# Pool weights fused between the first value tiles, and 16-row value tiles with high and low parts stacked

## The chip, the cores and the metric

The kernel runs on one core of a Trainium2 chip. Its time is the device time of one execution in microseconds (us). Times of before and after are medians of several executions; a profile is one further execution, recorded by the hardware profiler. The engines are PE (matmul), ACT, DVE and POOL (elementwise work), and SP, which here only issues the transfers (DMAs).

## What is computed

One hybrid decoder layer over 2064 tokens (16 meta tokens and 2048 others), width 1024:

```python
h = layer_norm(concat([meta, x]), ln_in_g, ln_in_b)
q, k, v, f_logit, g_att, u, g_pool = split(h @ w_in)
a = forgetting_attention(q, k, v, f_logit, b_forget) * silu(g_att)   # 16 heads of 64
p = multiscale_pool(u, w_pool, pool_scale) * silu(g_pool)            # 4 groups of 256
y = concat([a, p]) @ w_out
out = layer_norm(2**0.25 * h + y, ln_g, ln_b)[16:]
```

In the pool mixer a trailing mean and then a linear map w_pool act on u, which is itself a projection. Both are linear, so the kernel multiplies the u columns of w_in by w_pool first, group by group, and projects with the product. This is "fusing the pool weights".

## The kernel before

Every float32 matmul is made of three: an operand is split into a high part (rounded to the PE's reduced format by ACT) and a low part (the rest, by a subtraction on DVE or POOL), and high x high, high x low and low x high are summed (`mm3`, `split`). All compute instructions go through a helper at line 86 that fixes the order on PE, DVE, ACT and POOL as written; every profile row therefore has line L86, and is told apart by its tiles. Transfers on SP are not fixed by it: their order comes from the framework's own planner.

The change touches the first phase, up to the value projection (lines 189 to 401):

- **Fusing.** `fuse_load(g)` fetches the raw weights of pool group g: wpool (128x512, 256 KB) and two tiles of the transposed u columns (128x1024, 512 KB each) into a pool of their own, `fz`. `fuse_split` makes high and low parts (ph, pl, uh, ul), `fuse_mm(g)` runs 48 matmuls of 256 columns in four PSUM tiles and stores the product to `wupd`. The four groups run one after the other at the start (line 355); the splits of the next group, the LayerNorm of a token tile and the splits of the value weights stand between the matmuls. Then `fz` is closed and its memory goes to `hh` and `hl`.
- **LayerNorm.** `ln_load(i)` fetches a tile of 128 tokens (i = -1: the 16 meta tokens); `ln_norm(i)` takes statistics on DVE (bst, mv, rs, nb), normalizes on ACT, and applies gain and bias on POOL (xt<-xt,g_bc and xt<-xt,b_bc). `ln_turn(i)` transposes the tile on PE (tr<-ident,xt) and splits it into `hh` (ACT) and `hl` (DVE), columns 16+128i to 144+128i.
- **Value tiles.** `v_tile(half, wts, kt)` multiplies 128 tokens by 512 value columns: 24 matmuls of 512 columns (d<-wvh,hh and its two partners), then a split into a `vs` tile (two buffers, `vslot`) and a 512 KB store to `vd`. 2064 tokens make 16 full tiles and one of 16 rows; the 16-row tile takes 24 matmuls as well. Half 0 runs inside the loop at line 375 that also loads tile i+4, transposes tile i+1 and normalizes tile i+3. Half 1 follows at line 396.
- **Weights of half 1.** Eight 256 KB pieces through three staging buffers (`wst`); three are fetched ahead, one is split ahead of the 16-row tile of half 0, the other seven behind it.

After the value tiles come forget logits, the other projections, attention, output projection and the closing LayerNorm; none of that is touched.

Of the kernel before, what the change touches and what calls it, by code (L numbers as in the profile page):

```python
# [16 lines left out]
P = 128  # L17
NM = 16
# [22 lines left out]
def kernel(  # L41
# [147 lines left out]
    with ExitStack() as vscope:  # L189
        vpool = pool(vscope, "vpool")  # L190
# [21 lines left out]
        def ln_norm(i):  # L212
# [11 lines left out]
            nc.vector.scalar_tensor_tensor(  # L224
                out=nb[:n], in0=mv[:n, 0:1], scalar=-1.0, in1=rs[:n], op0=ALU.mult, op1=ALU.mult
            )
            nc.scalar.activation(
                out=xt[:n], in_=xt[:n], func=AF.Identity, scale=rs[:n], bias=nb[:n]
            )
            for op, row in ((ALU.mult, g_bc), (ALU.add, b_bc)):  # L230
                nc.gpsimd.tensor_tensor(out=xt[:n], in0=xt[:n], in1=row[:n], op=op)
# [26 lines left out]
        def v_tile(half, wts, kt):  # L258
            n = min(P, L - P * kt)
            ps = dense()  # L260
            sl = slice(P * kt, P * kt + n)
            for k in range(KT):
                mm3(ps[:n], hh[:, k, sl], hl[:, k, sl], wts[k][0], wts[k][1], k == 0, k == KT - 1)
            vs = vslot().rearrange("p (h a e) -> p h a e", h=8, a=2)
            pv = ps[:n].rearrange("p (h e) -> p h e", e=DH)
            split(vs[:n, :, 1, :], vs[:n, :, 0, :], pv)
# [5 lines left out]
        fscope = ExitStack()  # L272
        fz = pool(fscope, "fz", side="right")

        def fuse_load(g):
            wp = fz.tile([P, 2, 256], F32, tag="wp", name="wp", bufs=4)
            dma(wp, wpool[g])
            us = [wp]
            for k in range(2):
                us.append(fz.tile([P, D], F32, tag="wu", name="wu", bufs=8))  # L280
                dma(us[-1], wut[2 * g + k])
            return us

        def fuse_split(us, r):
            def one(i, u):
                shape, tag = ([P, 2, 256], "p") if i == 0 else ([P, D], "u")
                h_, l_ = (
                    fz.tile(shape, F32R, tag=tag + t, name=tag + t, bufs=2 if i == 0 else 4)
                    for t in "hl"
                )  # L290
                split(h_, l_, u, nc.gpsimd if i == 2 else None)
                r.append((h_, l_))

            return [lambda i=i, u=u: one(i, u) for i, u in enumerate(us)]

        def fuse_mm(g, ws, us, pieces):
            raw = [
                f32(vslot()) if g == 3 else fz.tile([P, D], F32, tag="o", name="o", bufs=6)
                for _ in range(2)
            ]  # L300
            os = [t.rearrange("p (k b e) -> p k b e", k=4, b=2) for t in raw]
            n = -(-len(pieces) // 4)

            def evac(kp, ps):
                pv = ps.rearrange("p (a b e) -> p a b e", a=2, b=2)
                dst = os[kp // 2][:, 2 * (kp % 2) : 2 * (kp % 2) + 2]
                if kp % 2:
                    nc.vector.tensor_copy(dst, pv)
                else:
                    nc.scalar.copy(out=dst, in_=pv)  # L310

            last = None
            for kp in range(4):
                ps = dense()
                for s in range(2):
                    dsl = slice(P * (2 * kp + s), P * (2 * kp + s + 1))
                    for k in range(2):
                        mm3(
                            ps[:, 256 * s : 256 * (s + 1)], us[k][0][:, dsl], us[k][1][:, dsl],
                            ws[0][:, k], ws[1][:, k], k == 0, k == 1,  # L320
                        )
                if last:
                    evac(*last)
                last = (kp, ps)
                for f in pieces[n * kp : n * (kp + 1)]:
                    f()
            evac(*last)
            for b in range(2):
                for q in range(2):
                    dma(wupd[2 * g + b][:, 4 * q : 4 * q + 4, :], os[q][:, :, b, :])  # L330
# [3 lines left out]
        raws = {0: fuse_load(0)}  # L334
# [7 lines left out]
        raws[3] = fuse_load(3)  # L342
        ln_load(2)
        sts = deque()
        for k in range(KT):
            sts.append(fz.tile([P, 512], F32, tag="wv", name="wv", bufs=KT))
            dma(sts[-1], wv[0, k])
        dma(wfs, wf)
        dma(bf_t, b_forget)
        dma(psc_t, pool_scale)  # L350
        hot = []
        for f in fuse_split(raws.pop(0), hot):
            f()
        wts = []
        for g in range(4):
            us = hot
            ws = us.pop(0)
            hot = []
            pieces = []
            if g + 1 < 4:  # L360
                pieces += fuse_split(raws.pop(g + 1), hot)
                pieces.append(lambda: ln_norm(g - 1))
            if g >= 2:
                pieces += [lambda: wts.append(wv_split(sts.popleft()))] * 4
            fuse_mm(g, ws, us, pieces)
        fscope.close()
        htp = pool(phase_a, "htp", side="right")
        hh = htp.tile([P, KT, L], F32R, tag="hh", name="hh")
        hl = htp.tile([P, KT, L], F32R, tag="hl", name="hl")
        ln_turn(-1)  # L370
        ln_load(3)
        ln_turn(0)
        ln_norm(2)
        split(wfr[:, :, 0:H], wfr[:, :, 32 : 32 + H], wfs)
        for i in range(NKT):
            if i + 4 < 16:
                ln_load(i + 4)
            if i + 1 < 16:
                ln_turn(i + 1)
            if i + 3 < 16:  # L380
                ln_norm(i + 3)
            if i == 14:
# [8 lines left out]
        wts = wts1  # L391
        for k in range(1, KT):
            wts.append(wv_split(sts.popleft()))
            if k + 3 < KT:
                sts.append(wv_load(1, k + 3))
        for kt in range(NKT):
# [4 lines left out]
            v_tile(1, wts, kt)  # L401

# [824 lines left out]
```

## Time and profile before

| | |
|---|---|
| time before, median of 3 | 2393.3 us (2392.06 to 2394.99) |
| the profiled execution's own time | 2390.21 us |
| its span | 2388.5 us |
| PE busy, share of the span | 2321.6 us, 97% |
| DVE / ACT / POOL busy | 60% / 40% / 30% |

The span runs from the first to the last recorded instruction. PE is TensorE's matmul row; since matmuls overlap, its recorded durations are longer than the distance from one start to the next, and the distance is what counts. "Idle before" a row is the time that its engine waited, with what released it behind the arrow. The granted clock is given as a share of the full 2.4 GHz; 0.5 is the lower level, 1.2 GHz.

### The profile page before, as it was taken

What the parts mean: (1) busy time and instruction counts of PE and PEld (TensorE: products, weight loads), DVE (VectorE), ACT (ScalarE), POOL (GpSimd) and SP (SyncE); (2) the same over time, 40 slices, a digit from 0 to 9 for tenths busy, and PEclk for the clock granted to TensorE, in tenths of its full rate; (3) what the DMA queues carried; (4) which work ended last, traced back from release to release, by engine and by line L of the source; (5) the groups of instructions that cost most, each with busy time, mean ns of one, the idle gap of its engine ahead of it and who ended that gap; (6) DMA issues with size and microseconds to landing.
All of it is one profiled execution on the core that took longest, in us unless ns stands there. A gap on an engine that the chain in (4) does not pass through costs nothing. (4 is left out here: it accounts for less than half of the span.)

```text
span 2388.5 us, 32719 instructions
## 1 busy us (share of the span) xinstructions
PE 2321.6 (97%) x11706; PEld 1922.0 (80%) x11706; DVE 1431.6 (60%) x2116; ACT 959.7 (40%) x1813; POOL 718.1 (30%) x528
## 2 busy tenths in 40 slices
PE   6999999999999999999999999999999999999998
PEld 5778798898988989888887767777777777776787
DVE  6641145644655456545535188787888878778357
ACT  4431221222212212121111387777778777776000
POOL 4730021212313404050001135353453535444000
PEclk8999999999999999999999999999999999999999
DMA  7853231222222222222212576575666657555955
GB/s 255 263 164 97 59 96 61 89 63 82 90 61 90 77 66 85 68 75 86 77 67 79 159 205 190 159 222 164 195 187 198 199 164 227 175 176 152 310 185 167
DMA packets 317506, 333.59 MB, mean 140 GB/s; under 512 B 27744, under 2 KB 241072, under 8 KB 317312
## 3 DMA queue, kind: packets, MB, share of 16 engines
q1 hardware_dynamic: 317344, 331.51, 45.5%
q8 instruction: 92, 1.51, 0.3%
q14 instruction: 70, 0.57, 0.1%
HBM read 207.43 MB, written 124.00 MB: 139 GB/s over the span
## 5 line engine op out<-in xcount | busy, mean ns | idle before, releaser
L86 PE MATMUL d<-hh,wh 128*128 128x412 f32 (+2 forms) x1472 | 561.2, 381 | 0.0
L86 PE MATMUL d<-hl,wh 128*128 128x412 f32 (+2 forms) x1472 | 538.6, 366 | 0.0
L86 PE MATMUL d<-hh,wl 128*128 128x412 f32 (+2 forms) x1472 | 538.6, 366 | 0.0
L86 DVE TENSOR_REDUCE mxs<-mx 128x1 f32<-128x912 f32 (+14 forms) x416 | 358.1, 864 | 279.7 <-PE mx L86 275.2
L86 DVE TENSOR_TENSOR pl<-s,ph 128x512 fp32r<-128x512 f32 (+2 forms) x576 | 374.6, 663 | 166.6 <-ACT s L86 153.5
L86 ACT ACTIVATE ph<-s 128x512 fp32r<-128x512 f32 (+2 forms) x576 | 334.6, 581 | 170.1 <-PE s L86 159.2
L86 PE MATMUL d<-wh,xm 128*128 128x512 f32 x1024 | 352.3, 400 | 5.1 <-DMA xm<-xa 5.1
L86 ACT ACTIVATE s<-s 128x512 f32<-128x512 f32 (+2 forms) x576 | 332.7, 578 | 0.0
L86 PEld LDWEIGHTS d<-hl,wh 128*128 128x128 f32 x1472 | 278.4, 189 | 23.1
L86 PEld LDWEIGHTS d<-hh,wl 128*128 128x128 f32 x1472 | 276.9, 188 | 23.5
L86 PEld LDWEIGHTS d<-hh,wh 128*128 128x128 f32 x1472 | 280.6, 191 | 18.2
L86 PE MATMUL s<-qa,ka 68*128 68x512 f32 (+4 forms) x704 | 258.1, 367 | 18.4 <-DVE pl L86 18.3
L86 POOL TENSOR_TENSOR wl<-wst,wh 128x1024 fp32r<-128x1024 f32 x40 | 96.2, 2405 | 576.0 <-ACT wh L86 575.9
L86 PE MATMUL s<-qb,kb 128*128 128x512 f32 (+4 forms) x704 | 244.8, 351 | 0.0
L86 PE MATMUL xo<-ph,vt 128*128 128x512 f32 (+3 forms) x640 | 232.9, 368 | 0.0
L86 POOL TENSOR_TENSOR tu<-ph 128x512 f32<-128x512 f32 x144 | 191.3, 1330 | 134.6 <-ACT ph L86 116.1
L86 PEld LDWEIGHTS d<-wh,xm 128*128 128x128 f32 x1024 | 192.3, 189 | 42.8 <-issue 4.9
L86 PE MATMUL yo<-pl,vt 128*66 128x512 f32 (+3 forms) x640 | 223.0, 365 | 0.5 <-ACT c L86 0.5
L86 PE MATMUL mx<-ka,qa 66*128 66x512 f32 (+5 forms) x704 | 200.2, 351 | 6.5 <-ACT qa L86 3.9
L86 PE MATMUL d<-wl,xm 128*128 128x512 f32 x512 | 204.3, 399 | 0.0
L86 PEld LDWEIGHTS s<-qa,ka 68*128 68x128 f32 (+1 forms) x704 | 127.7, 181 | 73.3 <-DVE pl L86 31.3
L86 PEld LDWEIGHTS mx<-ka,qa 66*128 66x128 f32 x704 | 133.0, 190 | 23.5 <-ACT qa L86 5.2
(140 smaller groups left out, 3049.2 us busy)
## 6 DMA issues: line engine op xcount, KB each, us to landing
xm<-xp SPq DMA_DIRECT2D x32, 1024.0 KB
xm<-xa SPq DMA_DIRECT2D x20, 1024.0 KB
vd<-vs SPq DMA_DIRECT2D x32, 512.0 KB
vt<-vd SPq DMA_DIRECT2D x64, 256.0 KB
qb<-kqd SPq DMA_DIRECT2D x64, 256.0 KB
xa<-am SPq DMA_DIRECT2D x32, 512.0 KB
xp<-pm SPq DMA_DIRECT2D x32, 412.0 KB
kqd<-lo SPq DMA_DIRECT2D x64, 206.0 KB
```

The costliest lines, as they stand in the source:

```text
L86: return in_order(f(*a, **k))
```

## The change

The pool `fz` goes. `hh` and `hl` are allocated at the start, and the split pool weights are kept in their last 1024 columns, which token tiles 8 and up fill later (`fuse_parts`: sixteen slots, five for a group). Raw pieces pass through the three `wst` buffers as 256 KB pieces (`fuse_feed`); the products are evacuated by ACT alone, 128x1024 at a time, into the `vs` buffers. Group 0 is fused first, from raw tiles that sit in a `wst` and both `vs` buffers; meta and token tile 0 are normalized ahead of its splits, tile 0's gain and bias are on DVE. Value tile 0 follows, and groups 1, 2 and 3 are fused ahead of value tiles 1, 2 and 3; the pieces of group g+1 are split behind the transposes of an iteration. The 16-row tiles use a stack `hs` of 48 columns (high part in 0 to 15, low part in 32 to 47, zeros between): 16 matmuls instead of 24, whose two row groups are added at the end; the low x low product is thereby included. Between the matmuls of the first of them, the weights of half 1 are split; two of these are now staged in another pool (`wq`). The forget weights are loaded and split later.

```diff
+        htp = pool(phase_a, "htp", side="right")
+        hh = htp.tile([P, KT, L], F32R, tag="hh", name="hh")
+        hl = htp.tile([P, KT, L], F32R, tag="hl", name="hl")
...
+        def v_rest(half, wts, hs, each):
+            ps = dense()
+            for k in range(KT):
+                for t in range(2):
+                    mm(
+                        ps[:48], hs[:, k, :], wts[k][t],
+                        start=k == 0 and t == 0, stop=k == KT - 1 and t == 1,
+                    )
+                each(k)
+            vf = wslot("wst")
+            nc.scalar.copy(out=vf[:NM], in_=ps[32:48])
+            nc.vector.tensor_tensor(out=vf[:NM], in0=ps[:NM], in1=vf[:NM], op=ALU.add)
+            v_out(half, NKT - 1, NM, vf[:NM])
...
+        def fuse_parts(g):
+            def slot(i):
+                i += 5 * (g % 3)
+                return (hh, hl)[i // KT][:, i % KT, L - D : L]
...
+        def fuse_feed(g):
+            parts = fuse_parts(g)
+            pieces = [(*parts[0], wpool[g])]
             for k in range(2):
...
+                for c in range(2):
+                    cs = slice(512 * c, 512 * (c + 1))
+                    pieces.append((parts[1 + k][0][:, cs], parts[1 + k][1][:, cs], wut[2 * g + k, :, cs]))
...
+            def step(i):
+                split(pieces[i][0], pieces[i][1], raw[i])
+                if i + 3 < 5:
+                    load(i + 3)
+
+            for i in range(3):
+                load(i)
+            for i in range(5):
+                step(i)
+            return parts
+
+        def fuse_mm(g, f, pieces):
+            ws, *us = f
+            pieces = deque(pieces)
+            for half in range(2):
+                ps = psm.tile([P, 1024], F32, tag="mx", name="fz", bufs=2)
...
+                    if pieces:
+                        pieces.popleft()()
+                o = f32(vslot())
+                nc.scalar.copy(out=o, in_=ps)
...
         ln_load(-1)
-        raws[1] = fuse_load(1)
         ln_load(0)
+        first = [wslot("wst").rearrange("p (k e) -> p k e", k=2), f32(vslot()), f32(vslot())]
+        for st, src in zip(first, (wpool[0], wut[0], wut[1])):
+            dma(st, src)
         bcast_row(g_bc, ln_in_g)
         bcast_row(b_bc, ln_in_b)
-        raws[2] = fuse_load(2)
+        wraw = lnp.tile([P, D], F32, tag="xt", name="wraw", bufs=4)
+        sts = deque(wraw[:, 512 * k : 512 * (k + 1)] for k in range(2))
+        for k in range(2):
+            dma(sts[k], wv[0, k])
+        sts.extend(wv_load(0, k) for k in range(2, 4))
         ln_load(1)
...
+        stats = [ln_stat(i) for i in (-1, 0)]
+        gains = [ln_apply(i, *stats[i + 1], nc.vector if i == 0 else None) for i in (-1, 0)]
+        fz = {0: fuse_parts(0)}
+        for (h_, l_), st in zip(fz[0], first):
+            split(h_, l_, st)
+        for f in gains:
             f()
         wts = []
...
+        def wv_next():
+            k = len(wts)
+            if k + 4 < KT:
+                sts.append(wv_load(0, k + 4))
+            wts.append(wv_split(sts.popleft()))
+
+        fuse_mm(0, fz.pop(0), [wv_next] * 4)
         ln_turn(-1)
+        ln_load(2)
+        ln_turn(0)
         ln_load(3)
-        ln_turn(0)
+        while len(wts) < KT:
+            wv_next()
+        ln_norm(1)
+        fz[1] = fuse_feed(1)
         ln_norm(2)
-        split(wfr[:, :, 0:H], wfr[:, :, 32 : 32 + H], wfs)
-        for i in range(NKT):
+        for i in range(NKT - 1):
+            if i in fz:
+                fuse_mm(i, fz.pop(i), [])
             if i + 4 < 16:
                 ln_load(i + 4)
-            if i + 1 < 16:
+            if 1 <= i < 15:
                 ln_turn(i + 1)
+            if 1 <= i < 3:
+                fz[i + 1] = fuse_feed(i + 1)
             if i + 3 < 16:
                 ln_norm(i + 3)
...
             if i == 14:
                 sts = deque(wv_load(1, k) for k in range(3))
-            if i == 16:
-                wts1 = [wv_split(sts.popleft())]
-                sts.append(wv_load(1, 3))
+            if i == 15:
+                w1 = [wv_split(sts.popleft())]
+                nc.scalar.copy(out=hs[:, :, 0:NM], in_=f32(hh[:, :, L - NM : L]))
+                nc.vector.tensor_copy(hs[:, :, 32:48], f32(hl[:, :, L - NM : L]))
             v_tile(0, wts, i)
-            if i == 15:
+            if i == 0:
+                ln_turn(1)
+            if i == 14:
                 lnscope.close()
                 wq = pool(phase_a, "wq", side="right")
...
+        def each(k):
+            if sts:
+                w1.append(wv_split(sts.popleft()))
+            if k + 5 < KT:
+                sts.append(wv_load(1, k + 5))
+
+        v_rest(0, wts, hs, each)
```

## Rows read from the trace of the kernel before

**Rows 1.** The page of the profile: busy us, share of the span and instructions of each engine.

```profile
PE 2321.6 (97%) x11706; PEld 1922.0 (80%) x11706; DVE 1431.6 (60%) x2116; ACT 959.7 (40%) x1813; POOL 718.1 (30%) x528
```

**Rows 2.** Stretches of the span, one row each: busy time and instructions of each engine, then PE's granted clock, the DMA share and GB/s.

```profile
0.00:60.00 60.00, 39.25 (x232) 35.71 (x233) 40.49 (x51) 29.29 (x45) 29.22 (x22) 0.89 0.75 256
60.00:100.00 40.00, 37.22 (x186) 30.40 (x185) 26.24 (x51) 18.40 (x32) 30.04 (x13) 1.00 0.84 270
166.50:177.40 10.90, 7.61 (x26) 4.34 (x25) 5.20 (x8) 4.61 (x8) 0.00 (x0) 1.00 0.36 103
```

**Rows 3.** Timeline of PE in the first 110 us: start, duration, operation, and idle time before it. d<-ph,uh and its partners are the matmuls of the pool groups, tr the transposes (those of 55.46, 64.31 and 97.44 are token tiles 1, 2 and 7).

```profile
10.61 0.58 PE L86 MATMUL d<-ph,ul 128*128 128x256 f32 x1 [1.63 <-POOL ul L86]
14.84 0.41 PE L86 MATMUL d<-ph,uh 128*128 128x256 f32 x1
15.05 0.36 PE L86 MATMUL d<-pl,uh 128*128 128x256 f32 x1
16.43 0.28 PE L86 MATMUL d<-ph,uh 128*128 128x256 f32 x1
16.55 0.28 PE L86 MATMUL d<-pl,uh 128*128 128x256 f32 x1
27.50 0.58 PE L86 MATMUL d<-ph,uh 128*128 128x256 f32 x1 [4.31 <-DVE o L86]
51.80 0.66 PE L86 MATMUL tr<-ident,xt 16*128 16x16 f32 x8
55.46 1.17 PE L86 MATMUL tr<-ident,xt 128*128 128x128 f32 x8 [1.05 <-DVE hl L86]
64.31 1.09 PE L86 MATMUL tr<-ident,xt 128*128 128x128 f32 x8 [2.12 <-POOL xt L86]
97.44 1.03 PE L86 MATMUL tr<-ident,xt 128*128 128x128 f32 x8
```

**Rows 4.** Groups of instructions up to 260 us, by shape: count | busy us, mean ns of one | idle before them. wv and wst are staged value weights, hl and hh the parts of the transposed tokens.

```profile
L86 POOL TENSOR_TENSOR xt<-xt,b_bc 128x1024 f32<-128x1024 f32 x16 | 39.0, 2438 | 1.3
L86 POOL TENSOR_TENSOR xt<-xt,g_bc 128x1024 f32<-128x1024 f32 x16 | 38.4, 2400 | 36.3 <-ACT xt L86 36.3
L86 DVE TENSOR_TENSOR hl<-tr,hh 128x512 fp32r<-128x512 f32 x32 | 20.5, 680 | 1.2 <-ACT hh L86 1.2
L86 ACT CAST hh<-tr 128x512 fp32r<-128x512 f32 x32 | 17.2, 594 | 1.3 <-PE tr L86 1.3
L86 ACT CAST uh<-wu 128x1024 fp32r<-128x1024 f32 x8 | 8.2, 1045 | 1.9 <-DMA wu<-in_wut_dram 1.9
L86 DVE TENSOR_TENSOR wvl<-wst,wvh 128x512 fp32r<-128x512 f32 x8 | 5.3, 683 | 4.1 <-ACT wvh L86 4.1
L86 ACT CAST wvh<-wst 128x512 fp32r<-128x512 f32 x8 | 4.7, 617 | 4.6 <-DMA wst<-in_wv_dram 4.5
```

**Rows 5.** Timeline of DVE in the first 75 us: start, duration, operation.

```profile
33.82 3.41 DVE L86 TENSOR_TENSOR ul<-wu,uh 128x1024 fp32r<-128x1024 f32 x1
37.15 1.27 DVE L86 BATCH_NORM_STATS2 bst<-xt 128x6 f32<-128x512 f32 x2
54.63 1.29 DVE L86 TENSOR_TENSOR hl<-tr,hh 128x512 fp32r<-128x512 f32 x2 [1.24 <-ACT hh L86]
71.05 0.53 DVE L86 SCALAR_TENSOR_TENSOR nb<-mv,rs 128x1 f32<-128x1 f32 x1
```

**Rows 6.** Timeline of POOL in the first 75 us.

```profile
33.43 2.72 POOL L86 TENSOR_TENSOR xt<-xt,b_bc 128x1024 f32<-128x1024 f32 x1
69.18 2.38 POOL L86 TENSOR_TENSOR xt<-xt,b_bc 128x1024 f32<-128x1024 f32 x1
```

**Rows 7.** Timeline of ACT in the first 75 us: the third split of group 0, and a normalization.

```profile
7.09 1.04 ACT L86 CAST uh<-wu 128x1024 fp32r<-128x1024 f32 x1 [0.76 <-DMA wu<-in_wut_dram]
39.48 1.24 ACT L86 ACTIVATE xt<-xt,nb,rs 128x1024 f32<-128x1024 f32 x1 [0.43 <-DVE nb L86]
```

**Rows 8.** Timeline of ACT from 148 us on: the end of half 0 and the start of half 1.

```profile
166.70 0.57 ACT L86 CAST vs<-d 16x512 fp32r<-16x512 f32 x1 [4.46 <-PE d L86]
175.25 0.62 ACT L86 CAST wvh<-wst 128x512 fp32r<-128x512 f32 x1 [1.42 <-DMA wst<-in_wv_dram]
177.42 0.59 ACT L86 CAST vs<-d 128x512 fp32r<-128x512 f32 x1 [1.55 <-PE d L86]
182.98 0.59 ACT L86 CAST vs<-d 128x512 fp32r<-128x512 f32 x1 [4.97 <-PE d L86]
```

**Rows 9.** Timeline of DVE in the same stretch.

```profile
171.96 1.34 DVE L86 TENSOR_TENSOR wvl<-wst,wvh 128x512 fp32r<-128x512 f32 x2 [2.17 <-ACT wvh L86]
183.60 0.69 DVE L86 TENSOR_TENSOR vs<-d,vs 128x512 fp32r<-128x512 f32 x1 [4.87 <-ACT vs L86]
```

**Rows 10.** Stretches of 0.5 us behind the DVE row of 183.60, when one store of a value tile is the only transfer: the last column is GB/s, the one before it the DMA share.

```profile
185.30:185.80 0.50, 0.50 (x4) 0.38 (x3) 0.00 (x0) 0.00 (x0) 0.00 (x0) 1.00 1.02 294
186.80:187.30 0.50, 0.50 (x4) 0.42 (x3) 0.00 (x0) 0.00 (x0) 0.00 (x0) 1.00 0.53 149
```

**Rows 11.** Timeline of PE at the end of half 1: the first and the last of the 24 matmuls of the 16-row tile.

```profile
260.62 0.40 PE L86 MATMUL d<-wvh,hh 128*16 128x512 f32 x1
265.95 0.39 PE L86 MATMUL d<-wvh,hl 128*16 128x512 f32 x1
```

**Rows 12.** Transfers of the first 100 us: GB/s in 40 slices of 2.5 us.

```profile
GB/s 27 381 338 415 408 405 408 405 401 389 386 343 296 280 4 0 105 0 0 80 286 212 225 356 324 224 243 333 107 300 383 185 370 246 321 224 137 357 236 326
```

More of the change, by code (lines that the diff above doesn't have):

```diff
@@ L210, in ln_load, with ln_stat @@
             xts[i] = xt
-        def ln_norm(i):
+        def ln_stat(i):
             n = NM if i < 0 else P
@@ L229, in ln_norm, with ln_gain @@
             )
+            return lambda: ln_gain(i, eng or nc.gpsimd)
+        def ln_gain(i, eng):
+            n = NM if i < 0 else P
+            xt = xts[i]
             for op, row in ((ALU.mult, g_bc), (ALU.add, b_bc)):
-                nc.gpsimd.tensor_tensor(out=xt[:n], in0=xt[:n], in1=row[:n], op=op)
+                eng.tensor_tensor(out=xt[:n], in0=xt[:n], in1=row[:n], op=op)
+        def ln_norm(i):
+            ln_apply(i, *ln_stat(i))()
         def ln_turn(i):
@@ L256, in wv_split, with v_out @@
             return h_, l_
[L258 to L263, printed above, removed]
+        def v_out(half, kt, n, pv):
             vs = vslot().rearrange("p (h a e) -> p h a e", h=8, a=2)
-            pv = ps[:n].rearrange("p (h e) -> p h e", e=DH)
-            split(vs[:n, :, 1, :], vs[:n, :, 0, :], pv)
+            split(vs[:n, :, 1, :], vs[:n, :, 0, :], pv.rearrange("p (h e) -> p h e", e=DH))
             dma(
@@ L270, in v_tile @@
             )
[L272 to L278, printed above, removed]
-            for k in range(2):
[L280 to L316, printed above, removed]
+        def v_tile(half, wts, kt):
+            ps = dense()
+            sl = slice(P * kt, P * (kt + 1))
+            for k in range(KT):
+                mm3(ps, hh[:, k, sl], hl[:, k, sl], wts[k][0], wts[k][1], k == 0, k == KT - 1)
+            v_out(half, kt, P, ps)
@@ new lines, in v_rest @@
+        def v_rest(half, wts, hs, each):
+            ps = dense()
+            for k in range(KT):
+                for t in range(2):
[8 more added lines that the diff above has]
+            v_out(half, NKT - 1, NM, vf[:NM])
@@ L317, in fuse_mm @@
+        def fuse_mm(g, f, pieces):
[3 more added lines that the diff above has]
+                ps = psm.tile([P, 1024], F32, tag="mx", name="fz", bufs=2)
+                for kd in range(4):
+                    dsl = slice(P * (4 * half + kd), P * (4 * half + kd + 1))
                     for k in range(2):
                         mm3(
-                            ps[:, 256 * s : 256 * (s + 1)], us[k][0][:, dsl], us[k][1][:, dsl],
+                            ps[:, 256 * kd : 256 * (kd + 1)], us[k][0][:, dsl], us[k][1][:, dsl],
@@ L320, in fuse_mm @@
                             ws[0][:, k], ws[1][:, k], k == 0, k == 1,
                         )
[L322 to L330, printed above, removed]
+                    if pieces:
+                        pieces.popleft()()
@@ L332 @@
+                o = f32(vslot())
+                nc.scalar.copy(out=o, in_=ps)
+                o = o.rearrange("p (k b e) -> p k b e", k=4, b=2)
+                for b in range(2):
+                    dma(wupd[2 * g + b][:, 4 * half : 4 * half + 4, :], o[:, :, b, :])
+            while pieces:
+                pieces.popleft()()
         wfs = vpool.tile([P, KT, H], F32, tag="wfs", name="wfs")
         nc.gpsimd.memset(f32(wfr), 0.0)
-        raws = {0: fuse_load(0)}
         ln_load(-1)
-        raws[1] = fuse_load(1)
@@ L353 @@
+        fz = {0: fuse_parts(0)}
+        for (h_, l_), st in zip(fz[0], first):
+            split(h_, l_, st)
+        for f in gains:
             f()
         wts = []
[L355 to L365, printed above, removed]
@@ L387 @@
             v_tile(0, wts, i)
-            if i == 15:
+            if i == 0:
+                ln_turn(1)
+            if i == 14:
                 lnscope.close()
                 wq = pool(phase_a, "wq", side="right")
[L391 to L396, printed above, removed]
+                v2 = pool(vscope, "v2")
+                hs = v2.tile([P, KT, 48], F32R, tag="hs", name="hs")
+                nc.gpsimd.memset(f32(hs), 0.0)
+                st = wq.tile([P, KT, P], F32, tag="wst", name="wst")
+                st = st.rearrange("p (a b) e -> p a (b e)", a=2)
+                for k in range(3, 5):
+                    dma(st[:, k - 3], wv[1, k])
+                    sts.append(st[:, k - 3])
@@ L397 @@
+        def each(k):
[4 more added lines that the diff above has]
+        v_rest(0, wts, hs, each)
+        wts = w1
+        for kt in range(NKT - 1):
             if kt == 8:
@@ L401 @@
             v_tile(1, wts, kt)
+        v_rest(1, wts, hs, lambda k: None)
     qscope = ExitStack()
```

34 lines of the change are left out of this document (19 added, 15 removed).

## The prediction

> **What bounds the kernel now.** I read the page's busy shares first, then the table of stretches, then the timelines of PE, DVE, POOL and ACT up to 260 us. PE is busy 97% of the span [rows 1], and all PE work stands in one written order, so time that is won or lost on PE in the first 270 us moves the end by as much; what follows is unchanged. Losses sit in two places. Up to 60 us PE is busy 39.25 us at a mean granted clock of 0.89 [rows 2]: each pool group waits some 4 us for its splits, as at 27.50, and restarts at the lower level [rows 3]. The first value tile comes after the transposes of 55.46, and those of 64.31 wait 2.12 us for POOL's gain [rows 3]. At the half change, 166.5 to 177.4, PE is busy 7.61 of 10.9 us [rows 2].
>
> **The half change and the 16-row tiles.** ACT takes up the last tile of half 0 at 166.70 and the first tile of half 1 at 177.42: 10.72 us, where the next tile takes 182.98 - 177.42 = 5.56 [rows 8]. PE waits for weights whose splits queue behind the 16-row tile, the last ones behind loads. The change has five raw pieces loaded by then and splits them between the 16-row tile's matmuls. By my count the sixth low part is ready 4.4 us after that tile starts and is wanted at 3.7 + 5 x 0.695 = 7.2. So 10.72 - 5.56 = 5.16 us go. A 16-row tile now takes 24 matmuls, (265.95 - 260.62)/23 = 0.232 us each [rows 11]; stacked, it takes 16. Their length doesn't follow the stationary columns here, since full tiles have the same 5.56/24. Two tiles: 2 x 8 x 0.232 = 3.71 us. The added ACT copy and DVE sum (about 0.6 and 0.7 us by rows of that size [rows 4]) lie beside PE: the next tile has the other PSUM buffer; uncovered they would cost 1.3 us. Copies into the stack and its memset lie in a tile where ACT and DVE idle most of 5.56 us: zero. The moved wfr load and split: zero for the same reason, 2.4 us at most if it meets POOL. Here the change wins 5.16 + 3.71 = 8.9 us; at the least, with the stall kept, 3.7.
>
> **The front, step by step.** PE's 192 pool matmuls and its transposes stay. What changes is what they wait for: ACT and DVE also keep their written order, so I follow their queues. Unit prices: a 512-wide split is 0.6 on ACT and 0.7 on DVE, a wide copy 1.05 [rows 4]; from the first statistics to the end of the normalization is 39.48 + 1.24 - 37.15 = 3.57 [rows 5, 7]; POOL's gain is 2.40 + 2.44 [rows 4]. A DVE operation with two SBUF operands waits for a running POOL operation: at 33.82 one lasts 3.41, ending 1.08 after POOL's end at 36.15; even the tiny nb of 71.05 waits for POOL's end [rows 5, 6]. They take turns. A load's hop, from the DVE operation that frees its slot (the first of the pair at 171.96, so 172.6) to ACT's use at 175.25, is 2.65 us [rows 8, 9]. A 512 KB store has its last byte about 2.8 us after its DVE operation (183.60 + 0.69 to some 187.05) [rows 9, 10]; with completion I take 3.2 (between 2.8 and 3.7).
>
> (a) Start. Meta and x tile 0 are now queued ahead of the pool weights. By the bytes per 2.5 us slice [rows 12] and about 1 us of completion (the third transfer, 1280 KB deep, is moved at 5.9 and used at 7.09 [rows 7, 12]), x tile 0 lands at 4.7 and g_bc at 9.9. Statistics and two normalizations occupy ACT to 9.2, then the three splits of group 0 come. DVE's three low parts (0.6 + 1.15 + 1.15) take turns with POOL's two gains of the meta tile, and the last is done at 17.5. (If g_bc lands after 10.7, one turn less: 15.4.) Then 48 matmuls of which five are through: 21 at the lower level, 0.21 apart, for 4.5 us, 22 at 0.12 [rows 3]: group 0 ends at 24.6.
>
> (b) Meta and tile 0 are transposed; before, 51.80 to 55.92 is 4.1 us [rows 3, 5]; now an evacuation stands ahead on ACT, 0.7 more: 29.4. Weight 4 is split until 30.05, and only that frees the slot of weight 7, which lands at 32.7 and is split at 34.05. Value tile 0 runs beside that, 28.5 to 34.2. But ln_norm(1) is written behind the weight 7 split on ACT and DVE: normalized at 37.6, first gain to 40.0, a turn of DVE, second gain to 42.8. The transposes of tile 1 and group 1 stand behind that on PE, which idles from 34.2 to 42.8.
>
> (c) Group 1's fourth piece needs a slot freed by its first, the fifth by its second (42.8 + 0.6 = 43.4): landed 46.05, split 47.4. ln_norm(2) ends on ACT at 51.0, its gains at 55.9. ln_norm(3)'s nb waits for POOL until 53.4, so that normalization ends at 54.75, and value tile 0, finished at 34.2, is evacuated only then, to 56.0.
>
> (d) From there a round repeats for groups 2 and 3, because two vs buffers serve both kinds of output and the second pool evacuation waits for the previous value tile's store: store 3.2, evacuation 1.05, high parts of the transposes 1.05, end of low parts 0.7, first split 0.6, load hop 2.65, fourth split 1.35, fifth 0.6, ln_norm 3.57, value evacuation 1.3: 16.1 us, where PE's own work is 48 x 0.12 + 1.1 + 5.6 = 12.4. So value tile 1 is evacuated at 72.1, tile 2 at 88.2. Behind them only store, evacuation and transposes: 94.2; ln_norm(6) ends at 97.8, its gains at 102.6. PE, freed by group 3's fifth piece at 83.3, has reached the same point at 101.8. Tile 6 transposed 103.7, value tile 5 to 109.3, transposes, value tile 6 starts at 110.4. Before, it starts behind the transposes of 97.44, at 98.5 [rows 3]. From there both run at the same pace. The front loses 11.9 us.
>
> (e) Seven hops of this chain (four loads, three stores) are priced from a stretch with a DMA share of 0.36; between 60 and 100 us it is 0.84 [rows 2], and more traffic joins there. No row times a hop under that load. Bounds: nothing, or 1.5 us each (a 512 KB store ahead in line: bytes moved for some 1.5 us [rows 10]), so 0 to 10.5. I take 0.2 each, nearest the measured hop, 1.4.
>
> The Trainium skill ("DMA: Bandwidth & Descriptors", Latency and other measured facts) says that HBM access takes 0.2 us on average and 2 us at high load. Our quiet hop of 2.65 can't tell; by that page's rule the seven hops could cost up to 7 x 1.8 = 12.6 us more (an estimate from the page), which would make the change 0.6% slower. That is the second rival's mechanism, priced there from rows.
>
> **Sum.** +11.9 + 1.4 - 8.9 = +4.4 us. The profiled execution took 2390.21 us; so 2394.6 for it. The median shown, 2393.3, is 3.1 above that execution; on it, 2397.7. Forecast 2397.5. A measurement of this kernel tells 0.2%, 4.8 us, from no change: 2388.5 to 2398.1.
>
> **Rivals.**
> First, faster: the queue chain doesn't bind, because ACT and DVE are free earlier than I count (g_bc late, loads landing early, slots freed sooner) and PE runs through. Then from 28.5 PE has 6 x 5.56 of value tiles, 7 x 1.09 of transposes and 3 x 5.7 of groups, so value tile 6 starts at 86.6, 11.9 us earlier than before; with the 8.9 that is 2372.5. Half way, with both rounds at PE's 12.4 (7.4 us less) and ln_norm(1) not held by weight 7 (34.05 - 29.4 = 4.65 less), the front of 11.9 falls to zero and the time is 2384. For it: PE idles long before the splits today and the new PE order has work to put there. Against it: in-order queues and two vs buffers are in the code.
> Second, slower: the hops. At 0.25 us each above quiet the sum passes 0.2%; at 1.5 each it is 11.9 + 10.5 - 8.9 = 13.5 us, 2407. For it speaks the DMA share of 0.84; against it, a round moves some 3.9 MB (x, hd, vd, five pieces, two stores) in 16.1 us, 240 GB/s, below the 270 of that stretch.
> Third, the change doesn't do what it says at the half change: the early loads of half 1 come late, and 5.2 us stay: 2403.
>
> **Chances.** Forecast's case 0.52, which straddles the limit: within 0.32, slower 0.20. First rival 0.26 (faster 0.24, same 0.02), second 0.17 and third 0.05 (both slower). Faster 0.24, same 0.34, slower 0.42. The likeliest case alone is 2392 to 2402; the range 2384 to 2407 takes in half of the first rival's way and nearly all of the second's.
>
> **What would show it.** Right: PE idle around 34 to 43 us behind POOL's gain of tile 1; value tile 0 evacuated some 20 us after its last matmul; ACT waiting for a vd store ahead of the second pool evacuation; the value tile after the transposes of tile 7 at about 110; one 3.7 us tile at the half change with no PE idle, and another at the end of half 1. Wrong: ln_norm(1) ready before value tile 0 ends, groups 2 and 3 starting as soon as a value tile ends, value tile 6 before 100, or a PE stall after the first 16-row tile.

## The result and the profile after

The changed kernel takes 2400.98 us (median of 11 executions, 2397.92 to 2403.87) against 2393.3 us before (11 executions beside them): ratio 1.0033, 95% interval 1.0025 to 1.0042. It is slower by 7.7 us. The profiled execution took 2401.14 us with a span of 2399.1.

The page of after, the row that answers to [rows 1]:

```profile
PE 2324.7 (97%) x11690; PEld 1927.7 (80%) x11690; DVE 1428.1 (60%) x2123; ACT 963.9 (40%) x1821; POOL 702.7 (29%) x523
```

The shares are the same, and there are 16 matmuls less: two 16-row tiles with 8 fewer each. The difference is in where PE waits. Two marks split the span: the transposes of the last token tile, and the first matmul of the forget logits. Before, by the timeline of PE:

```profile
148.94 1.04 PE L86 MATMUL tr<-ident,xt 128*128 128x128 f32 x8
...
266.19 0.35 PE L86 MATMUL d<-hh,wfr 128*48 128x416 f32 x1
```

And PE after (start, duration, operation, idle time before it; the transposes of 42.21, 56.26, 113.78 and 166.57 are token tiles 1, 2, 7 and 15, fz are the pool groups, hs is the stack):

```profile
15.15 7.20 PE L86 MATMUL fz<-hh 128*128 128x256 f32 x43 [2.28 <-DVE hh L86]
22.28 0.66 PE L86 MATMUL tr<-ident,xt 16*128 16x16 f32 x8
...
42.21 1.97 PE L86 MATMUL tr<-ident,xt 128*128 128x128 f32 x8 [7.38 <-POOL xt L86]
...
56.26 1.94 PE L86 MATMUL tr<-ident,xt 128*128 128x128 f32 x8 [5.29 <-DVE hl L86]
...
68.25 8.28 PE L86 MATMUL fz<-hl 128*128 128x256 f32 x45 [3.12 <-ACT hl L86]
...
113.78 1.03 PE L86 MATMUL tr<-ident,xt 128*128 128x128 f32 x8
127.88 1.09 PE L86 MATMUL tr<-ident,xt 128*128 128x128 f32 x8 [1.06 <-POOL xt L86]
...
166.57 1.04 PE L86 MATMUL tr<-ident,xt 128*128 128x128 f32 x8
178.56 0.39 PE L86 MATMUL d<-wvh,hs 128*48 128x512 f32 x1
...
182.03 0.39 PE L86 MATMUL d<-wvl,hs 128*48 128x512 f32 x1
...
274.91 0.35 PE L86 MATMUL d<-hh,wfr 128*48 128x416 f32 x1
```

The front costs 166.57 - 148.94 = 17.6 us. The half change and the 16-row tiles win (266.19 - 148.94) - (274.91 - 166.57) = 117.25 - 108.34 = 8.9 us. The rest of the span is 1.9 us longer (2399.1 - 274.91 against 2388.5 - 266.19). Together 17.6 - 8.9 + 1.9 = 10.6, the difference of the two spans.

The table of stretches after, for the front and for the half change [rows 2]:

```profile
0.00:60.00 60.00, 30.51 (x157) 26.07 (x158) 35.93 (x52) 24.37 (x37) 22.21 (x19) 0.83 0.67 219
60.00:100.00 40.00, 33.42 (x179) 29.64 (x179) 16.23 (x31) 17.40 (x27) 9.72 (x5) 0.87 0.74 228
...
166.50:188.00 21.50, 21.50 (x98) 16.54 (x97) 8.94 (x15) 8.33 (x16) 0.00 (x0) 1.00 0.61 184
```

In the first 60 us PE is busy 30.5 us where it was 39.25, at a lower granted clock; around the half change it no longer idles at all. Why PE waits in the front is read from ACT's timeline, where each wait for a transfer is named:

```profile
32.20 0.62 ACT L86 CAST wvh<-wst 128x512 fp32r<-128x512 f32 x1 [5.05 <-DMA wst<-in_wv_dram]
...
45.71 0.62 ACT L86 CAST hl<-wst 128x512 fp32r<-128x512 f32 x1 [2.57 <-DMA wst<-in_wut_dram]
60.09 1.01 ACT L86 COPY vs<-fz 128x1024 f32<-128x1024 f32 x1 [3.41 <-DMA vd<-vs]
67.58 0.62 ACT L86 CAST hl<-wst 128x512 fp32r<-128x512 f32 x1 [3.95 <-DMA wst<-in_wut_dram]
77.82 1.01 ACT L86 COPY vs<-fz 128x1024 f32<-128x1024 f32 x1 [3.17 <-DMA vd<-vs]
85.89 1.25 ACT L86 CAST hh<-wst 128x512 fp32r<-128x512 f32 x2 [4.52 <-DMA wst<-in_wut_dram]
95.94 1.02 ACT L86 COPY vs<-fz 128x1024 f32<-128x1024 f32 x1 [3.19 <-DMA vd<-vs]
```

And DVE's, which shows what each of these transfers waited for:

```profile
26.34 1.89 DVE L86 TENSOR_TENSOR wvl<-wst,wvh 128x512 fp32r<-128x512 f32 x3
32.85 0.69 DVE L86 TENSOR_TENSOR wvl<-wst,wvh 128x512 fp32r<-128x512 f32 x1 [4.63 <-ACT wvh L86]
...
54.82 0.69 DVE L86 TENSOR_TENSOR vs<-d,vs 128x512 fp32r<-128x512 f32 x1 [1.83 <-ACT vs L86]
62.83 1.89 DVE L86 TENSOR_TENSOR hl<-wst,hl 128x512 fp32r<-128x512 f32 x3
73.77 0.69 DVE L86 TENSOR_TENSOR vs<-d,vs 128x512 fp32r<-128x512 f32 x1 [1.78 <-ACT vs L86]
80.56 1.89 DVE L86 TENSOR_TENSOR hh<-wst,hh 128x512 fp32r<-128x512 f32 x3
91.86 0.69 DVE L86 TENSOR_TENSOR vs<-d,vs 128x512 fp32r<-128x512 f32 x1 [1.83 <-ACT vs L86]
115.17 2.34 DVE L86 TENSOR_TENSOR wfr<-wfs,wfr 128x128 fp32r<-128x128 f32 x1 [1.62 <-ACT wfr L86]
```

Read together they give the length of each hop, from the DVE operation that frees a slot or hands over a store to ACT's use. Loads: the first of three low parts is done 1.89/3 = 0.63 after 26.34, 62.83 and 80.56, so 32.20 - 26.97 = 5.2, 67.58 - 63.46 = 4.1 and 85.89 - 81.19 = 4.7 us; for group 1 (its second low part ends at some 42.6, by SP's issue of the load behind it) 3.1. Stores: 60.09 - 55.51 = 4.6, 77.82 - 74.46 = 3.4, 95.94 - 92.55 = 3.4. The forecast had priced 2.65 for a load and 3.2 for a store, so the seven are 8.3 us longer than quiet ones.

### The profile page after: what moved, and what is told of

It is laid out like the page before. It is cut to its first block, busy times and chain, and to the rows that moved or that the text cites. A ratio compares the mean times of both kernels' runs of the same rounds, so it can differ in the third digit from the quotient of the medians.

```text
span 2399.1 us, 32726 instructions
## 1 busy us (share of the span) xinstructions
PE 2324.7 (97%) x11690; PEld 1927.7 (80%) x11690; DVE 1428.1 (60%) x2123; ACT 963.9 (40%) x1821; POOL 702.7 (29%) x523
## 4 chain that ended last, share of the span: by engine, by line
PE 88%; DVE 4%; DMA 3%; ACT 2%; issue 2%; POOL 1%; SPq 0%; ACTq 0%; DVEq 0%; POOLq 0%
PE d L86 59%; PE s L86 11%; PE yo L86 7%; PE mx L86 6%; PE xo L86 5%; PE fz L86 1%; DMA wst<-in_wut_dram 1%; DVE pl L86 1%; POOL tu L86 1%; POOL araw L86 0%; ACT ph L86 0%; PE tr L86 0%; DVE bst L86 0%; DVE hl L86 0%; DMA xm<-xa 0%
```

## Experiments

Each ratio stands against the kernel before, run on the same chip. Its median was 2392.1 to 2393.3 us from one batch to the next, so a difference between medians of two batches is good to about 1 us.

**The half change alone.** Front of before; only the stacked 16-row tiles and the splits between their matmuls.

```diff
-            if i == 16:
-                wts1 = [wv_split(sts.popleft())]
-                sts.append(wv_load(1, 3))
...
+        v_rest(0, wts, hs, each)
...
+        v_rest(1, wts, hs, lambda k: None)
```

> The kernel before with only the stacked 16-row tiles and the splits of half 1 within the first of them; its front is untouched. Theory (the half change wins 8.9 us and the front alone loses): 2393.3 - 8.9 = 2384.4, and 108.3 us from the transposes of tile 15 to the first forget matmul, where the kernel before takes 117.25. Rival (the gain at the half change needs the new front, or is given back later): at most 3.7 us faster, 2389.6 or more.

2384.18 us, ratio 0.9967 (0.9954 to 0.9979). The timeline of PE has the forget logits 108.6 us behind the last transposes, as in the changed kernel:

```profile
149.63 1.03 PE L86 MATMUL tr<-ident,xt 128*128 128x128 f32 x8
...
258.23 0.35 PE L86 MATMUL d<-hh,wfr 128*48 128x416 f32 x1
```

So the gain, 117.25 - 108.6 = 8.65 us here, stands by itself, and the loss belongs to the front.

**Away with the store hops: three vs buffers.** The room comes from spare ninth buffers of the split weights.

```diff
-tag="vs", name="vs", bufs=2
+tag="vs", name="vs", bufs=3
```

> The changed kernel with three vs buffers instead of two (room from the spare weight buffers), nothing else; the second pool evacuation no longer waits for a value tile's store. Theory (the ACT and DVE queue sets the rounds): ACT's three waits for vd<-vs, 3.41 + 3.17 + 3.19 = 9.8 us, go, and the kernel takes 2401 - 9.8 = 2391, between 2389 and 2394. Rival (PE's longest wait, 7.4 us for POOL's gain of tile 1, and what follows it is the loss): that wait is untouched, so within 2 us of 2401.

2396.23 us, ratio 1.0016 (1.0007 to 1.0025): about 4.8 us of the 9.8 expected, above the theory's range and below the rival's. ACT's waits for value stores are gone (ahead of the last evacuation 2.13 us are left, without a releaser in the profile), but the waits for loads grew from 3.95 and 4.52 (timeline of ACT):

```profile
64.37 0.62 ACT L86 CAST hl<-wst 128x512 fp32r<-128x512 f32 x1 [4.35 <-DMA wst<-in_wut_dram]
...
80.87 0.62 ACT L86 CAST hh<-wst 128x512 fp32r<-128x512 f32 x1 [4.86 <-DMA wst<-in_wut_dram]
```

SP's timeline shows who stands ahead of the load: four stores of products that now come in a row.

```profile
56.35 4.12 SPq L86 DMA_DIRECT2D wupd<-vs  x4
60.58 1.63 SPq L86 DMA_DIRECT2D wst<-in_wut_dram  x2
```

**Away with the load hops: five staging buffers.**

```diff
-tag="wst", name="wst", bufs=3
+tag="wst", name="wst", bufs=5
...
-            for i in range(3):
+            for i in range(5):
                 load(i)
```

> The changed kernel with five staging buffers instead of three, so that weight 7 and the fourth and fifth pieces of a group are loaded before they are wanted; two vs buffers as before. Theory: ACT's waits for these loads (5.05 for weight 7, some 6 in group 1, 4.2 and 4.5 in groups 2 and 3) go, some 18 of 20 us on the time: 2384, between 2381 and 2389. Rival (the rounds are set by the stores or by PE): the waits for stores grow by what the loads leave, 5 us faster at most, 2396.

The room comes from the same spare buffers. 2387.37 us, ratio 0.9977 (0.9968 to 0.9986): 13.6 us below the changed kernel, inside the range. ACT has no wait for a staged piece of groups 1 to 3 any more; the waits for value stores stay (timeline of ACT):

```profile
53.02 1.01 ACT L86 COPY vs<-fz 128x1024 f32<-128x1024 f32 x1 [3.44 <-DMA vd<-vs]
```

One buffer count takes most of the front's loss away: the load hop was its largest part.

**Is it PE's longest wait?** The LayerNorm of token tile 1 is written ahead of the splits of weights 4 to 7.

```diff
+        ln_norm(1)
         while len(wts) < KT:
             wv_next()
-        ln_norm(1)
```

> The changed kernel with ln_norm(1) ahead of the splits of weights 4 to 7 instead of behind them, nothing else. It removes most of PE's longest wait, the 7.4 us for POOL's gain of tile 1. Theory (ACT and DVE have the same work and the same waits for loads in sum, only in another order): tile 2 and the later rounds come when they came, 2399 to 2401. Rival (the longest PE wait is what is lost): 3.5 to 7 us faster, 2394 to 2397.5.

2401.36 us, ratio 1.0037 (1.0024 to 1.0049), 0.4 above the theory's range and far from the rival's. PE's wait of 7.38 us is gone, and nothing is won (timeline of PE):

```profile
38.85 1.07 PE L86 MATMUL tr<-ident,xt 128*128 128x128 f32 x8
...
113.01 1.03 PE L86 MATMUL tr<-ident,xt 128*128 128x128 f32 x8
```

The transposes of tile 1 start 3.4 us earlier, those of tile 7 only 0.8: PE now waits 3.74 us for a piece of group 1 instead, for whose load ACT waits 3.58. With three staging buffers the longest wait of the engine that ends last was slack in front of a chain on other engines.

**Filling the load waits with LayerNorms.** A LayerNorm is put between the third and the fourth piece of a feed, where ACT waited for the load.

```diff
+        fz[1] = fuse_feed(1, lambda: ln_norm(2))
...
+                if i == 3:
+                    between()
                 step(i)
```

> The changed kernel with work written into its load waits, no buffer added: ln_norm(1) stands between the splits of weights 6 and 7, and in each feed the LayerNorm that followed it stands between the third and the fourth piece. Theory (the front is ACT's and DVE's queue, its waits for loads included): of each of the four load waits up to one LayerNorm, 3.6 us, is covered, 13 us in all, less what the store waits grow: 2388 to 2392. Rival (a load's hop is paid once per group whatever stands before it, since the store waits take it up): 2398 or more.

2403.25 us, ratio 1.004 (1.0027 to 1.0053). The theory fell. ACT's waits for loads did go in groups 2 and 3 (in group 1 one of 3.79 us is left), but the low parts on DVE came under POOL's gains of the LayerNorm that had been moved ahead (timeline of DVE; two such low parts take 1.29 in rows where POOL is idle):

```profile
67.47 5.21 DVE L86 TENSOR_TENSOR hl<-wst,hl 128x512 fp32r<-128x512 f32 x2 [1.81 <-ACT hl L86]
```

PE's matmuls of the group wait for them, and by its place ACT's evacuation of the product waits for those (timeline of ACT; "issue" means that the profile shows no releaser):

```profile
74.77 1.01 ACT L86 COPY vs<-fz 128x1024 f32<-128x1024 f32 x1 [6.32 <-issue]
```

A wait of one engine was filled with work that takes another engine's turn.

**Both of the last ideas**, three vs buffers and this order:

> The order of the experiment before and three vs buffers. Theory: both kinds of wait are off the queue, and what three buffers alone gave back to the loads is covered too: 2396.2 - 13 = 2383, between 2380 and 2387. Rival (the stores and loads collide on the transfer queue, so one of the two is always waited for): no better than either alone, 2388 or more.

2397.21 us, ratio 1.0018 (1.001 to 1.0027). Again the rival's number: as with three buffers alone. Its reason is shown only in part: ACT's evacuations wait 3.30 and 4.66 us behind low parts that stand under POOL's gains (3.71 and 3.96 us for two), as in the experiment before, and beside that ACT waits 1.39 and 1.14 us for loads in groups 2 and 3.

**Why are the hops long?** The stores of the normalized token tiles 1 to 5 leave the front; rows of tiles 8 to 12 are stored in their place later, so the traffic in sum stays, and the right rows of tiles 1 to 5 are left out.

```diff
-            if i >= 0:
+            if i >= 0 and not 1 <= i <= 5:
                 dma(hd[P * i : P * (i + 1), :], xt)
+            if 8 <= i <= 12:
+                dma(hd[P * (i - 7) : P * (i - 6), :], xt)
```

> The changed kernel, but the stores of the normalized token tiles 1 to 5 (hd, 512 KB each) leave the front: their rows are stored with tiles 8 to 12, from those tiles, so hd holds wrong rows and the total traffic stays the same. Theory (the front lost more than forecast because the loads' hops in its chain, 4.3 us on average instead of the 2.65 priced, wait behind other transfers, the 512 KB store of the tile just transposed first of all): the loads of groups 1 to 3 land about 1 us earlier each, ACT's waits for staged pieces shrink by as much, the transposes of tile 7 start at 109 to 112 instead of 113.8, and the time is 2 to 5 us below the changed kernel, 2396 to 2399. Rival (the hops are that long by themselves, whatever else moves): within 1 us of the changed kernel, 2400 to 2402, with the same waits on ACT.

2397.79 us, ratio 1.0023 (1.0014 to 1.0033), as the theory had it. Timeline of ACT:

```profile
57.90 1.01 ACT L86 COPY vs<-fz 128x1024 f32<-128x1024 f32 x1 [2.21 <-DMA vd<-vs]
64.78 0.62 ACT L86 CAST hl<-wst 128x512 fp32r<-128x512 f32 x1 [3.34 <-DMA wst<-in_wut_dram]
...
81.66 0.62 ACT L86 CAST hh<-wst 128x512 fp32r<-128x512 f32 x1 [3.15 <-DMA wst<-in_wut_dram]
```

With the same working as above the loads of groups 2 and 3 take 3.5 and 3.3 us instead of 4.1 and 4.7, and the first store 3.4 instead of 4.6. The transposes of tile 7 start 3.9 us earlier than at 113.78 (timeline of PE):

```profile
109.87 1.03 PE L86 MATMUL tr<-ident,xt 128*128 128x128 f32 x8
```

Above the quiet prices the six hops of groups 1 to 3 had 5.75 us in the changed kernel and have 2.1 here: nearly two thirds was one kind of transfer ahead of them in line. What makes up the rest wasn't tried. The load of weight 7, the longest hop, isn't touched by this: ACT waits 4.93 us for it, 5.05 in the changed kernel.

**Is it the clock?** PE gets matmuls that nobody reads, ahead of the places where it idled.

```diff
+        def spin(n):
+            tp = pst.tile([P, 512], F32, tag="tr", name="spin", bufs=2)
+            for _ in range(n):
+                mm(tp, wts[0][0][:, 0:P], wts[0][1], start=True, stop=True)
```

> The changed kernel with idle work on PE, whose results nobody reads: 28 matmuls of 512 columns ahead of the transposes of tile 1, 16 ahead of those of tile 2, 9 ahead of groups 2 and 3 each, about as much as PE idles there (7.4, 5.3, 3.1 and 3.2 us). Theory (ACT's, DVE's and the transfers' chain sets the front; PE's granted clock there, 0.83 in the first 60 us and 0.87 in the next 40, costs nothing because PE waits for that chain anyway): the granted clock rises, the time stays, 2399.5 to 2402.5, and the transposes of tile 7 start within 1 us of 113.8. Rival (a good part of the front's loss is matmuls that run at the lower level after each wait): the transposes of tile 7 start 3 us or more earlier, 2394 to 2398.

2401.9 us, ratio 1.004 (1.0027 to 1.0053). The granted clock rose (stretches, the third column from the right), to 0.94 from 0.83 and to 0.91 from 0.87:

```profile
0.00:60.00 60.00, 33.43 (x174) 27.85 (x175) 36.04 (x52) 24.36 (x37) 18.65 (x18) 0.94 0.61 203
60.00:100.00 40.00, 37.32 (x208) 32.70 (x207) 13.72 (x26) 15.52 (x24) 12.24 (x6) 0.91 0.70 220
```

and nothing was won: the time is inside the theory's range. In the profiled execution (2405.84 us) tile 7 starts at 118.12, which misses the expected 113.8 by 4.3. Of that, 2.65 lies ahead of the first added matmul, in group 0 (the meta tile's transposes start at 24.93, not 22.28). The 16 matmuls ahead of tile 2's transposes did not fill the wait: they write the transposes' PSUM buffers, waited for DVE as those had, and ran behind the wait. The other rows are group 0 and group 2:

```profile
17.34 7.65 PE L86 MATMUL fz<-hh 128*128 128x256 f32 x43 [2.29 <-DVE hh L86]
...
59.38 5.87 PE L86 MATMUL spin<-wvl,wvh 128*128 128x512 f32 x16 [6.56 <-DVE hl L86]
...
73.58 5.77 PE L86 MATMUL fz<-hl 128*128 128x256 f32 x48
```

From the meta tile's transposes to tile 7 it is 93.2 us, against 91.5 in the changed kernel. Of these 1.7 us up to 1.42 are the place of the 16 matmuls: so long ACT waits for the transposes behind them. The clean reading lies behind that: group 2's matmuls run at the full clock, 5.6 us from the first to the next transposes (73.58 to 79.18) where the changed kernel's 45 take 8.1 (68.25 to 76.36), and yet the round from value tile 1's evacuation to value tile 2's takes 18.0 us, against 18.1. So in group 2's round the lower clock was a mark of the waiting and not the cause of the loss; group 3 still waited 2.68 us and ran at the lower clock, so there it wasn't tried.

**Towards a better version.** Five staging buffers, and the evacuations of a pool product written behind the transposes and the feed of its iteration:

```diff
-                o = f32(vslot())
-                nc.scalar.copy(out=o, in_=ps)
...
+                late.append(lambda half=half, ps=ps: fuse_out(g, half, ps))
```

> Five staging buffers, and the evacuations of groups 1 to 3 written behind the transposes and the feed of their iteration, so that a value tile's store has landed by then; no third vs buffer. Theory: ACT's three store waits (3.4, 3.2, 3.2) are covered; but with five buffers PE is within some 3.5 us of its own work from group 2 on, so 2387.4 - 3 = 2384, between 2382 and 2387. Rival (the queue still sets the time): all 9.8 us come back, 2378.

2385.31 us, ratio 0.997 (0.9958 to 0.9981), inside the range; the executions overlap with those of 2387.37, so the time alone doesn't settle the gain. ACT's waits for stores haven't gone but moved: 1.29 us for a value store and 2.21, 1.57 and 3.46 ahead of value tiles, for the products' stores. PE no longer waits for them; from tile 2's transposes to tile 7's its timeline names no wait, and tile 7 comes 1.9 us earlier than with five staging buffers alone (98.54):

```profile
96.60 1.09 PE L86 MATMUL tr<-ident,xt 128*128 128x128 f32 x8 [1.81 <-POOL xt L86]
```

To it the LayerNorm of tile 1 ahead of weights 4 to 7, and the split of the forget weights moved from token tile 5 to 15:

> The kernel before this one with ln_norm(1) ahead of weights 4 to 7 and the split of the forget weights moved from iteration 5 to iteration 15. Theory: now that the queue no longer sets the time, PE's wait for tile 1 counts, which it didn't with three buffers: 2.5 us for it and 1 us for the forget weights' split, which waits for POOL and delays a LayerNorm: 2384 - 3.5 = 2380.5. Rival (order still doesn't matter): 2384.

2387.51 us, ratio 0.9978 (0.9969 to 0.9987): not the gain expected, and 2 us worse than without; the loads of group 1, issued later, are waited for again (3.16 and 2.88 us on ACT). Only the forget weights moved:

> Five staging buffers and pool evacuations written behind the transposes and the feed, as measured before at 2385.3, and now the split of the forget weights moved from token tile 5 to tile 15, with nothing else changed. Theory (that split's subtraction waits for POOL and holds up a LayerNorm, which cost the changed kernel 1.06 us at the transposes of a later tile): 0.5 to 2 us faster than 2385.3, that is 2383 to 2385, and PE has no wait for POOL's gain behind tile 7. Rival (PE is caught up by the value tiles' own pace and nothing comes of it): 2385 to 2387. The version with only the half change, 2384.2, is the one to beat.

2384.37 us, ratio 0.9962 (0.9948 to 0.9976). The median is where the theory put it, but the executions overlap with those of 2385.31, so the gain isn't settled. The wait for POOL's gain behind tile 7, 1.15 us at 110.85 in the version before, is gone as expected, but in this profiled execution the tile before it ran partly at the lower clock and ate that (last section). Last, gain and bias of tile 1 go to DVE:

```diff
-        ln_norm(1)
+        ln_apply(1, *ln_stat(1), nc.vector)()
```

> The version with five staging buffers, deferred pool evacuations and the late split of the forget weights (2384.4), with one more edit: gain and bias of token tile 1 on DVE instead of POOL. Theory (DVE's low parts of group 1 and POOL's gain of tile 1 take turns, 5.79 us for three low parts that need 1.9 alone, and this turn is a part of the chain that sets the front): on DVE the two take 2 x 1.15 and then the low parts run free, so the transposes of tile 1 start at 35 to 36 instead of 37.75, the LayerNorm of tile 2 and what follows come about 2 us earlier, and the time is 1 to 3 us lower, 2381.5 to 2383.5. Rival (another wait ends the front, the one of 2.19 us for POOL's gain at tile 7): 2384 to 2386, with that wait longer by what was won before.

2380.98 us, ratio 0.9959 (0.9945 to 0.9972). The low parts of group 1 on DVE, in the version without this edit:

```profile
33.06 5.79 DVE L86 TENSOR_TENSOR hh<-wst,hh 128x512 fp32r<-128x512 f32 x3 [1.82 <-ACT hh L86]
```

and with it, then PE's transposes of tiles 1 and 7:

```profile
34.75 1.89 DVE L86 TENSOR_TENSOR hh<-wst,hh 128x512 fp32r<-128x512 f32 x3
```

```profile
34.98 1.07 PE L86 MATMUL tr<-ident,xt 128*128 128x128 f32 x8 [3.67 <-DVE xt L86]
...
94.83 1.09 PE L86 MATMUL tr<-ident,xt 128*128 128x128 f32 x8 [2.17 <-POOL xt L86]
```

The low parts end at 36.64 instead of 38.85, tile 1 comes 2.8 us earlier (37.75 before this edit) and tile 7 2.25 (97.08), the 2 us of the theory; the wait that the rival names stayed as it was (2.17 us, 2.19 before this edit). The median lies 0.5 below the theory's range, but the executions (2379.94 to 2386.17) overlap with those of 2384.37 (2380.67 to 2385.26), so the gain is shown by the trace and not settled by the times. This version has the lowest median of all. Its interval overlaps with that of the half change alone too, so which of these is the better isn't settled; both beat the kernel before and the changed one.

## Why the prediction was right, and where its size was off

The forecast was 2397.5 us in a range of 2384 to 2407, with 0.42 for slower, the largest of the three chances; measured 2400.98, slower by more than the 0.2% that can be told. Its reason, a loss in the front that the gain at the half change doesn't pay for, is what the runs show. Two things were luck. The forecast's own number, 4.4 us up, lies below the 4.8 that can be told; slower was the largest chance only with the second and third rivals added, and it was the second's mechanism that came. And the number is as near as it is because an early start hid part of what the hops cost more.

**Half change and 16-row tiles: 8.9 forecast, 8.9 measured** in the changed kernel, 8.65 alone. The stack's 16 matmuls run from 178.56 to 182.03, 3.47/15 = 0.231 us apart, the price of [rows 11]. The third rival is out.

**(a) Start.** The branch in brackets came: group 0's last matmuls start at 15.15 (forecast 15.4 in brackets, 17.5 without), and it ends at 22.3, not 24.6. Of the 12 profiled executions with this front, 11 took this branch (15.15 to 15.47); the one with the added matmuls took the other, 17.34. The step stood on where a broadcast lands relative to a DVE operation, so it is open from one execution to the next, and 2 us hang on it.

**(b), (c) Up to value tile 0.** Weight 7 was used at 32.20 (its split, low part included, was to end at 34.05, and ended at 33.54), POOL was done for tile 1 at 42.2 (forecast 42.8), value tile 0 was evacuated by 55.51 (forecast 56.0). Weight 4's low part, which frees the slot, was done at 26.97, 3.1 us earlier than the 30.05 of the forecast; the load of weight 7 took 5.2 instead of 2.65 and ate 2.6 of that.

**(d) The rounds.** The chain is the one that was written down: store, evacuation, transposes, splits, load, LayerNorm, value evacuation. Value tile 1 is evacuated at 73.77 + 0.69 = 74.46 and tile 2 at 92.55, rounds of 18.95 and 18.1 us instead of 16.1. Five staging buffers take the loads out of this chain, and 13.6 us go.

**(e) The hops, the step that failed in size.** The forecast allowed 0.2 us each, 1.4 in all, "nearest the measured hop"; the seven are 8.3 longer, 1.2 each, inside the bounds of 0 to 10.5. The earlier start hid part of it: by the forecast's own marks the chain is 0.5 early at value tile 0, then 4.85 late by the rounds, and value tile 6 starts at 114.8 where 110.4 stood without hops and 111.8 with them. So the term was worth 8.3 and not 1.4; 3.1 of it was paid by the start, and the rest of the chain came out 0.8 shorter. The bound of 1.5 us for a 512 KB store ahead in line was the better price: taking those stores away gave 3.9 us back at tile 7. This is the second rival's mechanism, at less than its upper price.

The Trainium skill's figures ("DMA: Bandwidth & Descriptors", Latency and other measured facts) had given up to 12.6 us for these hops as an estimate. The 8.3 measured lie below it, and part of them is waiting in line, which that figure doesn't name.

**The moved forget weights, priced at zero with 2.4 at most.** Their subtraction at 115.17 takes 2.34 us, ends with POOL's operation and delays a LayerNorm; PE waits 1.06 for it at 127.88. It cost that, not zero.

**A reading too wide.** The prediction says that each pool group of the kernel before waits some 4 us for its splits. PE's timeline has such a wait ahead of two of the four groups, 4.31 us at 27.50 and 4.49 at 40.10, and names DVE's evacuation of a product (`o`), which stood behind the splits in DVE's order. No term of the sum rests on it.

**The sum.** In profiled executions: 16.3 at tile 7, 1.1 at the forget weights, 0.2 unassigned, less 8.9, plus 1.9 in the rest of the span, which no step of the change touches and whose cause is open (that stretch takes 2122.3 us in the kernel before, 2123.4 with the half change alone and 2124.2 in the changed kernel, one execution each). The medians differ by 7.7, less than the 10.9 of the two profiled executions, because the one of before lay 3.1 below its median.

**The first rival**, a chain that doesn't bind, fell for this kernel. Five staging buffers and deferred evacuations bring its half-way case, a front that costs nothing (2384 us): tile 7 then comes at 96.60, where it was 97.44 before. Its full 11.9 us of gain no version came near; the best wins 2.6 at tile 7 (94.83).

## What to carry to other kernels

When a fill stage is interleaved with the main loop, follow the in-order queues of the elementwise engines and the transfers between them, not PE's waits: as long as three staging buffers set the pace the longest PE wait was worth nothing, while two more buffers were worth 13.6 us. Only behind that did shortening the same wait bring tile 7 forward, by 2.25 us. Price a transfer's hop with the transfers that stand ahead of it in the same stretch, since the quiet hops of another stage were shorter than every one of the seven in this chain. Before a wait is filled with other work, look at which second engine that work holds up.

## What the runs showed of the hardware

DVE's low parts and POOL's gains take turns operation by operation, and DVE is the loser: three low parts take 5.79 us beside POOL's gains and 1.89 without, 3.9 us more, where POOL's second gain takes 2.67 instead of 2.36. Moving the gains to DVE (2 x 1.23 us instead of 2.4 + 2.7 on POOL) ended the low parts 2.2 us earlier. The Trainium skill ("SBUF — State Buffer", Summary: rules for kernel authors) says that of a DVE operation with two SBUF inputs and a POOL operation that reads SBUF the second to issue waits for the first; the trace agrees: at 51.27 in the changed kernel even a 128x1 operation of DVE lasts 1.72 us, to the end of POOL's gain at 52.98. What it adds is the price, which here made the gains cheaper on the engine that was already the busier one.

Much the same wait of PE at tile 7 was followed by a lower clock in some profiled executions and not in others. Stretches behind it, in the version with the forget weights late and in the last one:

```profile
97.00:105.10 8.10, 8.02 (x32) 6.54 (x33) 4.00 (x9) 4.22 (x6) 5.18 (x4) 0.79 0.71 227
```

```profile
94.80:101.30 6.50, 6.47 (x32) 5.40 (x33) 4.00 (x8) 3.09 (x6) 4.82 (x2) 1.00 0.63 187
```

PE had waited 2.19 and 2.17 us. The granted clock was 0.79 in the first, part of it at the lower level of 1.2 GHz, and 1.00 in the second; from one tile's transposes to the next it took 8.03 and 6.49 us. The version with the LayerNorm moved ahead waited 2.03 us there and took 8.06 at 0.79, so the length of the wait doesn't tell which it will be. So 1.5 us can hang on a wait that looks the same, which is as much as some of these edits were worth.
